# Starting both feature groups of a recurrence's input projection on x's first two chunks, and turning six of x's eight chunks with VectorE blocks

## The chip, the cores and the metric

The kernel runs on one core of one Trainium2 chip. The metric is the device time of one execution in microseconds (us); lower is better. A core has five engines that run their own instruction streams and wait for each other through semaphores: TensorE (PE, matrix multiply; its weight loads are listed as PEld), VectorE (DVE), ScalarE (ACT), GpSimd (POOL) and SyncE (SP, which here only issues transfers). Transfers run on 16 DMA engines, which all queues share.

## The reference, cut to what matters

One layer of a hybrid encoder: an RMS norm of x, one wide projection, attention on one part of it, a gated linear recurrence (LRU) on another, a gated mix, and an output projection. x is 512 tokens by 2048 features, all float32.

```python
h = rms_norm(x, norm_w)
proj = jnp.einsum('bsd,de->bse', h, w_in)
q, k, v, g_attn, xr, g_lru = jnp.split(proj, SPLITS, axis=-1)
attn_out = attention_group(q, k, v, q_norm_w, k_norm_w)
lru_out = lru_group(xr, conv_w, conv_b, lru_wa, lru_ba, lru_wx, lru_bx, lru_lambda)
mixed = jnp.concatenate([rms_norm(attn_out, attn_norm_w) * jax.nn.silu(g_attn),
                         rms_norm(lru_out, lru_norm_w) * jax.nn.silu(g_lru)], axis=-1)
return x + jnp.einsum('bse,ed->bsd', mixed, w_out)
```

The change touches only the start: the projection to `xr`, the recurrence's input (1024 features, split into two groups of 512).

## The kernel before, in words

**Products.** Every float32 factor is held as two parts, a rounded high part and a low rest, and a product is three matmuls (`mm3`, L152 to L155): high by high, high by low, low by high. `wsplit` (L216) makes the two parts of a piece of weights: ScalarE writes `wh` (L223), VectorE writes `wl` (L224). x's two parts are kept as tiles named `x` (tag `x2`), 16 high and 16 low ones, each 128 features by 512 tokens. The norm's row factor is not in them: it is the vector `rbc`, multiplied in when a group's sums leave the accumulators.

**Chunks.** x's 2048 features are worked through in eight chunks of 256 (two slices of 128, called k). A chunk of x is loaded by `xload` (L245) with tokens on the partitions, as a tile named `b`, and must be turned so that features lie on the partitions. There are two ways. For the first `TURNED` = 5 chunks `xturn` (L254) has TensorE transpose eight 128x128 blocks against the identity `ident` (L258); ScalarE takes the high part out of the accumulator (L263) and VectorE the low part (L266). For chunks 5, 6 and 7 VectorE transposes 32x32 blocks in four instructions (`blocks`, L286) into a tile `xu`; `put_aside` (L294) writes it to DRAM (`xd`) in one transfer, and `bring_back` (L301) reads it in four transfers into another `xu` so that the blocks lie in order; ScalarE scales it by `norm_w` (L343) and writes the high part, VectorE the low part (both L344). `xsquare` makes the sums of squares for the norm, on VectorE for the first five chunks (L277), on ScalarE for the others (L273).

**The first group.** `proj_feat` (L385) runs over the chunks; per chunk 24 matmuls of 128x512 go into the four accumulators of the group. For the first two chunks the matmuls stand in an order of their own (L394), so that each starts as soon as its part is there. It yields after every 6 matmuls, and at such a step `moves` (L1206) says which loads, turns and splits are written there. Group 1 (`a1`) is done over all eight chunks; then group 2 (`a2`) over all eight, woven with the recurrence of group 1 (`lru_half`), then the projection to keys and values, woven with the recurrence of group 2.

**What sets the order.** TensorE's program is in the order written, throughout. At the start the same holds for SP (the `with` of `s1`, L1171), and for ScalarE and VectorE up to step (1, 2) (`s2`, closed at L1236); elsewhere a planner orders an engine's instructions by priorities. Each engine, and SP as the queue of the transfers, runs its program in order: an instruction that waits holds up those behind it. A raw weight tile `wr` comes from a ring of three, the split parts `wh` and `wl` from four buffers each. There are two sets of four accumulator banks, `pj` and `mm`.

**Small things at the start.** GpSimd makes the identity `ident` (a memset and a select out of `make_identity`, listed under masks.py) and a few constants. `norm_w` comes in as 16 rows, `nw_st`, and is turned by one transpose (`columns`, L194). `vec_load` (L185) loads seven small vectors (104 rows of 128 numbers) into `vec_st`, which is turned in the same way.

Of the kernel before, what the change touches and what calls it, by code (L numbers as in the profile page):

```python
# [11 lines left out]
F32 = mybir.dt.float32  # L12
# [40 lines left out]
TURNED = 5  # L53
# [10 lines left out]
def hybrid_kernel(  # L64
# [172 lines left out]
    highs, x_parts, squared = {}, [], []  # L237
# [16 lines left out]
    def xturn(xc, kk, then=None):  # L254
        pt = mm()
        for t in range(NT):
            ks = slice(kk % 2 * P, (kk % 2 + 1) * P)
            nc.tensor.transpose(pt[:, t * P : (t + 1) * P], xc[:, t, ks], ident)  # L258
        if then:
            then()  # L260
        xh[kk], xl[kk] = x2(), x2()
        with behind(split_done[-1] if kk > 3 else ()):
            highs[kk // 2] = nc.scalar.activation(  # L263
                xh[kk], pt, AF.Identity, scale=nw[:, kk : kk + 1]
            ).ins
        nc.vector.scalar_tensor_tensor(  # L266
            xl[kk], pt, nw[:, kk : kk + 1], f(xh[kk]), op0=ALU.mult, op1=ALU.subtract
        )

    def xsquare(xc, c):  # L270
        for t in range(NT):
            if c >= TURNED:
                nc.scalar.activation(  # L273
                    xc[:, t, :], xc[:, t, :], AF.Square, accum_out=ssq[:, t, c : c + 1]
                )
                continue
            square = nc.vector.scalar_tensor_tensor(  # L277
                xc[:, t, :], xc[:, t, :], 1.0, xc[:, t, :], op0=ALU.mult, op1=ALU.mult,
                accum_out=ssq[:, t, c : c + 1],
            )  # L280
            if c == 1:
                squared.append(square.ins)
# [25 lines left out]
    def xchunk(c):  # L308
        with tc.high_priority(AHEAD):
            (xc,) = xload(c)  # L310
        yield
        if c < TURNED:
            with tc.high_priority(AHEAD):
                for k in range(2):
                    xturn(xc, 2 * c + k)
            if c == 2:
                yield
            with behind(split_done[2][1:] if c == 2 else ()):
                xsquare(xc, c)
            yield  # L320
            return
        u, back = (
            ring.tile([P, NQ, 2, NT, B], F32, name=nm("xu")) for ring in (aring, hring)
        )
        with tc.high_priority(AHEAD), tc.issue_after(squared[-1] if c == TURNED else split_done[3][1]):
            for t in range(NT):
                blocks(u, t, xc[:, t, :])
        yield
        with tc.high_priority(AHEAD):
            there = put_aside(u, "xd", KT // 2 - TURNED)  # L330
        with tc.issue_after(highs[TURNED - 1]):
            xsquare(xc, c)
        yield
        with tc.high_priority(AHEAD):
            bring_back(back, there)
        yield
        with tc.high_priority(AHEAD), behind(split_done[-1]):
            for k in range(2):
                kk = 2 * c + k
                xh[kk], xl[kk] = x2(), x2()  # L340
                hi, lo = (in_order(v) for v in (xh[kk], xl[kk]))
                v = back[:, :, k]
                nc.scalar.activation(v, v, AF.Identity, scale=nw[:, kk : kk + 1])  # L343
                x_parts[:] = nc.scalar.copy(hi, v).ins, nc.vector.tensor_sub(lo, v, f(hi)).ins  # L344
        yield
# [11 lines left out]
    def rows(dst, col, dg):  # L357
# [14 lines left out]
        pb = mm()  # L372
# [4 lines left out]
    def xstats():  # L377
        s = const([P, NT], "xsum")
        nc.vector.reduce_sum(s, ssq, axis=AX.X)
        rsqrt_mean(rstd, s, DM, NT)  # L380
        yield from rows(rbc, rstd, lambda: k2(F32R, (P, NT, P)))
# [3 lines left out]
    def proj_feat(c0, acc, first=None, given={}, take=None):  # L385

        acc += [pj() for _ in range(4)]
# [93 lines left out]
    def lru_half(half, acc):  # L481
# [11 lines left out]
        xrs = evac_bc(acc)  # L493
        for b in range(0, 4, 2):
            bs = slice(b, b + 2)
            steps = ((6, 4, 8, 4), (10, 5, 8, 5))[half][bs]
            yield from lru_pair(4 * half + b, xrs[bs], grs[bs], steps, 99 if half and b else 0)

    def lru_pair(n0, xrs, grs, steps, rest):
# [23 lines left out]
        for b, n in enumerate((n0, n0 + 1)):  # L523
# [4 lines left out]
            for dst, j0, bias in ((rs[b], 0, R_BA), (is_[b], 2, R_BX)):  # L528
                for d in range(2):
                    pg = mm()  # L530
# [641 lines left out]
    s1.enter_context(tc.manual_schedule(engines={mybir.EngineType.SP}))  # L1172
# [5 lines left out]
    with tc.high_priority():  # L1178
# [12 lines left out]
        xturn(xc, 0, split_first)  # L1191
        busy(WARM2)
    stats = xstats()
    chunks = [xchunk(c) for c in range(1, KT // 2)]

    raws = {}

    def fetch_x(c):
        with tc.high_priority(AHEAD):
            (raws[c],) = wraw(w_in, c * 2 * P, C_XR)  # L1200

    def split_x(c):
        with tc.high_priority(AHEAD), behind(x_parts):
            given[c] = [wsplit(raws[c], k) for k in range(2)]

    moves = {  # L1206
# [6 lines left out]
    }  # L1213

    def move(step):
        for name in moves.get(step, "").split():
            n = int(name[1])
            if name[0] == "x":
                next(chunks[n - 1])
            else:  # L1220
                (fetch_x if name[0] == "w" else split_x)(n)

    for step in proj_feat(C_XR, a1, first, given):
        if step is None:
            with tc.high_priority():
                first.append(wsplit(raw, 1, nc.vector.tensor_copy))
                xturn(xc, 1)
            xsquare(xc, 0)
            move(None)
            given[1] = wload(w_in, 2 * P, C_XR)  # L1230
            continue
        c, e = step
        move(step)
        if (c, e) == (1, 2):
            s2.close()
        if (c, e) == (4, 2):  # L1236
            with tc.high_priority(AHEAD):
                vec_load()
        if (c, e) == (7, 1):
            columns(vec, vec_st)  # L1240
        if (c, e) in ((4, 3), (KT // 2 - 1, 0)):
            with tc.high_priority(AHEAD), tc.issue_after(split_done[-1][1]):
                next(stats)

# [3 lines left out]
    fill = proj_feat(C_XR + SEQ, a2)  # L1248
# [9 lines left out]
    fill = with_sums(fill, 8, 16)  # L1258
    weave(fill, lru_half(0, a1))
# [200 lines left out]
```

## Time and profile before

| | us |
|---|---|
| median of 3 runs | 626.39 (626.31 to 626.44) |
| profiled execution | 626.48 |
| its span on the core | 624.7 |
| TensorE busy | 620.0 (99%), 2756 matmuls |
| VectorE, ScalarE, GpSimd busy | 495.3, 352.4, 101.8 |
| mean transfer rate over the span | 204 GB/s |

The profiled execution is 1.8 us longer than its span (what lies before and after) and within 0.1 us of the median. All times in views are counted from the span's start. A row of a timeline has the start, the duration, the engine, the line of the kernel, the operation, what it writes and reads, and how many instructions it merges.

### The profile page before, as it was taken

Reading aid. Unit: us, or ns where it says so; the run is one execution under the profiler, and the core shown is the slowest. Engines: PE = TensorE matmul, PEld = TensorE weight load, DVE = VectorE, ACT = ScalarE, POOL = GpSimd, SP = SyncE. Lnnn points to the kernel's source line nnn. Section 1 sums busy time; section 2 is a strip of 40 time slices with the busy share of each in tenths; the row PEclk is TensorE's granted clock in tenths of the full one; section 3 lists DMA queues with packets and bytes.
Section 4 is the critical chain, followed back from the end, with each engine's and each line's share of the span. In section 5 each row is a group of like instructions: output and inputs, shape, how many; then the busy total and the mean of one; then the engine's idle time right before and its main releaser. Section 6 shows DMA issues by size and latency. Waiting matters only on the chain.

```text
span 624.7 us, 8293 instructions
## 1 busy us (share of the span) xinstructions
PE 620.0 (99%) x2756; PEld 512.6 (82%) x2756; DVE 495.3 (79%) x800; ACT 352.4 (56%) x617; POOL 101.8 (16%) x135
## 2 busy tenths in 40 slices
PE   9999999999999999999999999999999999999997
PEld 7888888888888888888888888888888888888886
DVE  5958979986699876887887888549979866887776
ACT  3675799479946833545485548338345633443441
POOL 0000210112003622622123223100210101010010
PEclk9999999999999999999999999999999999999999
DMA  8878686759774599479659646932995777897252
GB/s 285 277 210 271 178 202 171 175 135 195 239 235 137 170 247 240 100 204 270 192 173 258 201 137 192 256 91 76 283 254 184 216 250 242 288 333 230 68 202 101
DMA packets 74026, 127.61 MB, mean 204 GB/s; under 512 B 6664, under 2 KB 29312, under 8 KB 73984
## 3 DMA queue, kind: packets, MB, share of 16 engines
q1 hardware_dynamic: 66096, 109.65, 56.7%
q0 software_dynamic: 7712, 17.31, 14.3%
q8 instruction: 21, 0.34, 0.2%
q14 instruction: 21, 0.17, 0.1%
q10 hardware_dynamic: 176, 0.14, 0.1%
HBM read 110.29 MB, written 37.75 MB: 237 GB/s over the span
## 4 chain that ended last, share of the span: by engine, by line
PE 99%; DVE 0%; issue 0%
PE pj L154 20%; PE pj L155 20%; PE pj L153 20%; PE mm L1040 14%; PE pj L1040 11%; PE mm L155 4%; PE mm L154 3%; PE mm L153 3%; PE pj L394 2%; PE mm L258 1%; PE mm L1167 1%; PE mm L836 0%; DVE cb L1069 0%; PE mm L194 0%; PE mm L373 0%; DVE ones L159 0%
## 5 line engine op out<-in xcount | busy, mean ns | idle before, releaser
L153 PE MATMUL pj<-x,wh 128*128 128x512 f32 x368 | 143.5, 390 | 0.0
L155 PE MATMUL pj<-x,wl 128*128 128x512 f32 x368 | 143.2, 389 | 0.0
L154 PE MATMUL pj<-x,wh 128*128 128x512 f32 x368 | 143.2, 389 | 0.0
L223 ACT CAST wh<-wr 128x512 fp32r<-128x512 f32 x142 | 84.5, 618 | 81.5 <-PE pj L154 29.8
L224 DVE TENSOR_TENSOR wl<-wr,wh 128x512 fp32r<-128x512 f32 x144 | 98.5, 712 | 20.5 <-ACT wh L223 19.2
L888 ACT CAST wh<-wr 128x1024 fp32r<-128x1024 f32 (+1 forms) x72 | 60.6, 860 | 75.3 <-PE mm L1040 36.0
L889 DVE TENSOR_TENSOR wl<-wr,wh 128x1024 fp32r<-128x1024 f32 (+1 forms) x72 | 68.6, 983 | 29.0 <-ACT wh L888 28.9
L153 PEld LDWEIGHTS pj<-x,wh 128*128 128x128 f32 x368 | 69.1, 188 | 14.4
L154 PEld LDWEIGHTS pj<-x,wh 128*128 128x128 f32 x368 | 69.1, 188 | 14.3
L155 PEld LDWEIGHTS pj<-x,wl 128*128 128x128 f32 x368 | 69.1, 188 | 14.3
L154 PE MATMUL pj<-wl,x 128*128 128x512 f32 x192 | 74.7, 389 | 0.0
L155 PE MATMUL pj<-wh,x 128*128 128x512 f32 x192 | 74.7, 389 | 0.0
L153 PE MATMUL pj<-wh,x 128*128 128x512 f32 x192 | 74.7, 389 | 0.0
L912 POOL DMA_DIRECT2D t<-in_w_out_dram x40 | 33.6, 907 | 156.0 <-DMA t<-in_w_out_dram 96.9
L1040 PE MATMUL mm<-wh,ml 128*128 128x512 f32 x126 | 49.0, 389 | 0.0
L1040 PE MATMUL mm<-wh,mh 128*128 128x512 f32 x126 | 49.0, 389 | 0.0
L1040 PE MATMUL mm<-wl,mh 128*128 128x512 f32 x126 | 49.0, 389 | 0.0
L153 PEld LDWEIGHTS pj<-wh,x 128*128 128x128 f32 x192 | 36.0, 188 | 7.6
L154 PEld LDWEIGHTS pj<-wl,x 128*128 128x128 f32 x192 | 36.0, 188 | 7.5
L155 PEld LDWEIGHTS pj<-wh,x 128*128 128x128 f32 x192 | 36.0, 188 | 7.4
L712 POOL TENSOR_SCALAR p<-p,sm 128x512 f32<-128x512 f32 x32 | 24.2, 761 | 89.4 <-DVE sm L711 89.4
L1040 PE MATMUL pj<-wl,mh 128*128 128x512 f32 (+1 forms) x100 | 38.5, 385 | 0.0
(205 smaller groups left out, 1052.9 us busy)
## 6 DMA issues: line engine op xcount, KB each, us to landing
wr<-in_w_in_dram SPq DMA_DIRECT2D x71, 512.0 KB, 5.0
wr<-in_w_out_dram SPq DMA_DIRECT2D x21, 512.0 KB, 5.1
t<-in_w_out_dram POOLq DMA_DIRECT2D x40, 256.0 KB, 7.1
wr<-t SPq DMA_DIRECT2D x40, 256.0 KB, 5.8
pd<-u SPq DMA_DIRECT2D x16, 512.0 KB, 3.0
pt<-pd SPq DMA_DIRECT2D x64, 128.0 KB, 4.1
t<-in_w_out_dram SPq DMA_DIRECT2D x24, 256.0 KB, 5.3
wr<-in_w_out_dram SPq DMA_DIRECT2D x22, 256.0 KB, 4.2
```

The costliest lines, as they stand in the source:

```text
L153: nc.tensor.matmul(acc, lh, rh, start=start, stop=False)
L154: nc.tensor.matmul(acc, lh, rl, start=False, stop=False)
L155: nc.tensor.matmul(acc, ll, rh, start=False, stop=stop)
L223: copy(hi, raw[:, k, :]).ins,
L224: nc.vector.tensor_sub(lo, raw[:, k, :], f(hi)).ins,
L258: nc.tensor.transpose(pt[:, t * P : (t + 1) * P], xc[:, t, ks], ident)
L394: nc.tensor.matmul(acc[e], w[:, e * P : (e + 1) * P], x_[2 * c + k], start=c == k == j == 0, stop=False,)
L712: last_pool[0] = nc.gpsimd.tensor_scalar(p, p, sm, 0.0, op0=ALU.mult, op1=ALU.add).ins
L888: nc.scalar.copy(hi[:, to], b)
L889: nc.vector.tensor_sub(lo[:, to], b, f(hi[:, to]))
L912: nc.gpsimd.dma_start(dst, src, accum_op=ALU.add)
L1040: nc.tensor.matmul(dst[s][:, es], lh[:, ts_], rh[:, es], start=i == ends_[0] and j == 0, stop=i == ends_[1] and j == 2,)
```

## The change

- Two chunks instead of five are transposed by TensorE (`TURNED` = 2); chunks 2 to 7 go through VectorE's blocks, DRAM and back. Their sums of squares are made on ScalarE.
- After group 1's matmuls on chunks 0 and 1, group 2's matmuls on chunks 0 and 1 stand in TensorE's program (eight steps of 6 matmuls, drawn from `fill` by `islice`), then group 1's chunks 2 to 7, then group 2's. For this group 2 has the accumulators `mm` and group 1's gates `pj`.
- `vec_load` issues its seven loads from GpSimd's queue, where `moves` has the letter G, instead of SP's at step (4, 2); GpSimd's program is in the order written as well (`s1`). The vectors are turned at step (1, 3), and the recurrence's constants follow early on VectorE.
- ScalarE's and VectorE's programs are in the order written up to step (6, 0). The table `moves` now has a letter for each act (loads of x L, of weights W and F, turning T and H, squares Q, splits S and P, blocks B, put aside D, bring back R, making the parts V, the norm Z).
- The norm's broadcast takes a bank of `pj`, freed by a copy of the first accumulator (`done`).

```diff
-TURNED = 5
+TURNED = 2
...
-            nc.sync.dma_start(vec_st[lo : lo + src.shape[0], :], src)
+            nc.gpsimd.dma_start(vec_st[lo : lo + src.shape[0], :], src)
...
+    def block_x(c):
+        units[c] = [ring.tile([P, NQ, 2, NT, B], F32, name=nm("xu")) for ring in (aring, hring)]
+        for t in range(NT):
+            blocks(units[c][0], t, chunk[c][:, t, :])
+    def aside_x(c):
+        units[c][0] = put_aside(units[c][0], "xd", KT // 2 - TURNED)
+    def back_x(c):
+        bring_back(units[c][1], units[c][0])
+    def whole_x(c):
+        for k in range(2):
+            v = units[c][1][:, :, k]
+            nc.scalar.activation(v, v, AF.Identity, scale=nw[:, 2 * c + k : 2 * c + k + 1])
+        for k in range(2):
...
+            nc.scalar.copy(hi, v)
+            nc.vector.tensor_sub(lo, v, f(hi))
...
-        pb = mm()
+        pb = pj()
...
-    s1.enter_context(tc.manual_schedule(engines={mybir.EngineType.SP}))
+    s1.enter_context(tc.manual_schedule(engines={mybir.EngineType.SP, mybir.EngineType.Pool}))
...
+    def vectors(_):
+        with tc.issue_after(split_done[-1][1]):
+            vec_load()
...
+        None: "Q0 L1 W1 S1 L2 F0 L3 F1 G0",
+        (0, 2): "T1 H1 H1 B2 D2 P0 L4 L5 R2",
...
+    fill = proj_feat(C_XR + SEQ, a2, given=next_given, bank=mm)
+    done = []
     for step in proj_feat(C_XR, a1, first, given):
...
+        if step == (1, 3):
+            columns(vec, vec_st)
+            for c, e in itertools.islice(fill, 8):
+                move((c, e, 1))
...
-    fill = with_sums(fill, 8, 16)
-    weave(fill, lru_half(0, a1))
+    fill = with_sums(fill, 8, 8)
+    weave(fill, lru_half(0, a1, done))
```

GpSimd's program, from its first instruction of the kernel proper. Before:

```order
masks.py:197 MEMSET ident 128x128
L163 MEMSET ones_r 128x128
masks.py:199 ISA
masks.py:199 AFFINE_SELECT ident<-ident 128x128
L165 MEMSET nhalf 128x48
```

And after:

```order
L185 DMA vec_st<-in_conv_w_dram 32x128
L185 DMA vec_st<-in_conv_b_dram 8x128
L185 DMA vec_st<-in_lru_ba_dram 16x128
L185 DMA vec_st<-in_lru_bx_dram 16x128
L185 DMA vec_st<-in_lru_lambda_dram 16x128
L185 DMA vec_st<-in_attn_norm_w_dram 8x128
L185 DMA vec_st<-in_lru_norm_w_dram 8x128
masks.py:197 MEMSET ident 128x128
L163 MEMSET ones_r 128x128
masks.py:199 ISA
masks.py:199 AFFINE_SELECT ident<-ident 128x128
```

The seven loads stand ahead of the two instructions that make the identity, and wait for nothing; the planner put them there, though the code writes them later.

SP's program where the first chunk is put aside and brought back. `xd` is the DRAM tile, `xu` the tile in blocks (the source of `xd`) and in order (its reader), `b` a chunk of x, `wr` raw weights. Before, with chunk 5's `xd` first, then those of 6 and 7:

```order
L294 DMA xd_405<-xu_337 128x1024
L211 DMA wr_411<-in_w_in_dram 128x2x512
L301 DMA xu_338<-xd_405 32x4x256 x4
L211 DMA wr_417<-in_w_in_dram 128x2x512
L294 DMA xd_437<-xu_425 128x1024
L294 DMA xd_443<-xu_431 128x1024
L301 DMA xu_426<-xd_437 32x4x256 x4
L211 DMA wr_489<-in_w_in_dram 128x2x512
L301 DMA xu_432<-xd_443 32x4x256 x4
```

And after, for chunks 2, 3, 4 and the put-aside of 5:

```order
L294 DMA xd_255<-xu_249 128x1024
L244 DMA b_42_265<-in_x_dram 128x4x256
L244 DMA b_43_267<-in_x_dram 128x4x256
L301 DMA xu_250<-xd_255 32x4x256 x4
L294 DMA xd_295<-xu_289 128x1024
L211 DMA wr_297<-in_w_in_dram 128x2x512
L301 DMA xu_290<-xd_295 32x4x256 x4
L244 DMA b_52_327<-in_x_dram 128x4x256
L294 DMA xd_354<-xu_348 128x1024
L211 DMA wr_382<-in_w_in_dram 128x2x512
L301 DMA xu_349<-xd_354 32x4x256 x4
L294 DMA xd_414<-xu_408 128x1024
```

Six chunks instead of three go this way, one behind the other: each chunk's four reads wait for its own write, and the next chunk's write and weights stand behind those reads.

TensorE's program at the seam between the two groups, after the change. `pj` are group 1's accumulators, `mm_54` group 2's first, `wh_23` chunk 1's weights for group 1 and `wh_38` chunk 0's for group 2:

```order
L398 MATMUL pj_12_167<-x2_34_244,wh_23_198 128x512
L398 MATMUL pj_13_168<-x2_34_244,wh_23_198 128x512
L194 MATMUL mm_53_335<-ident_84,vec_st_97 128x104
L153 MATMUL mm_54_338<-x2_8_156,wh_38_257 128x512
L154 MATMUL mm_54_338<-x2_9_157,wh_38_257 128x512
```

48 matmuls of group 2 stand here between group 1's chunks 1 and 2; before, group 1's chunk 2 followed.

More of the change, by code (lines that the diff above doesn't have):

```diff
@@ L261, in xturn @@
         xh[kk], xl[kk] = x2(), x2()
[L262 to L265, printed above, removed]
+        yield
+        nc.scalar.activation(xh[kk], pt, AF.Identity, scale=nw[:, kk : kk + 1])
+        yield
         nc.vector.scalar_tensor_tensor(
@@ L268, in xturn @@
         )
+        yield
     def xsquare(xc, c):
@@ L306, in in_order @@
         return v.rearrange("p (t i r) -> p i t r", t=NT, i=NQ)
[L308 to L345, printed above, removed]
@@ new lines, in hybrid_kernel, with load_x, turn_x, step_x @@
+    chunk, squares, halves, units = {}, {}, {}, {}
+    def load_x(c):
+        (chunk[c],) = xload(c)
+        squares[c] = xsquare(chunk[c], c)
+    def turn_x(c):
+        halves[c] = [xturn(chunk[c], 2 * c + k) for k in range(2)]
+        step_x(c)
+    def step_x(c):
+        for half in halves[c]:
+            next(half)
+    def square_x(c):
+        drain(squares[c])
+    def block_x(c):
+        units[c] = [ring.tile([P, NQ, 2, NT, B], F32, name=nm("xu")) for ring in (aring, hring)]
+        for t in range(NT):
+            blocks(units[c][0], t, chunk[c][:, t, :])
@@ L380, in xstats, with proj_feat @@
         rsqrt_mean(rstd, s, DM, NT)
+        yield
         yield from rows(rbc, rstd, lambda: k2(F32R, (P, NT, P)))
-    def proj_feat(c0, acc, first=None, given={}, take=None):
-        acc += [pj() for _ in range(4)]
+    def proj_feat(c0, acc, first=None, given={}, take=None, bank=pj):
+        acc += [bank() for _ in range(4)]
         for c in range(KT // 2):
@@ L479, in evac_bc, with lru_half @@
         return res
-    def lru_half(half, acc):
+    def lru_half(half, acc, done=()):
         grs = []
@@ L496, in lru_half, with lru_pair @@
             steps = ((6, 4, 8, 4), (10, 5, 8, 5))[half][bs]
-            yield from lru_pair(4 * half + b, xrs[bs], grs[bs], steps, 99 if half and b else 0)
-    def lru_pair(n0, xrs, grs, steps, rest):
+            yield from lru_pair(4 * half + b, xrs[bs], grs[bs], steps, 99 if half and b else 0, mm if half else pj)
+    def lru_pair(n0, xrs, grs, steps, rest, bank):
         xcs, cs, rs, is_, ths = [], [], [], [], []
```

90 lines of the change are left out of this document (54 added, 36 removed), and 6 rows, old and new, of the table moves.

## Prediction

> **What bounds the kernel now.** I read the page first (engines, chain), then the chain in order of time, then the timelines of GpSimd, SP, ScalarE and VectorE over the first 60 us.
>
> ```profile
> PE 620.0 (99%) x2756; PEld 512.6 (82%) x2756; DVE 495.3 (79%) x800; ACT 352.4 (56%) x617; POOL 101.8 (16%) x135
> PE 99%; DVE 0%; issue 0%
> ```
>
> TensorE carries 99% of the chain. In order of time (start, duration, what):
>
> ```profile
> 1.04 2.74 PE mm L1167 x12
> 4.00 1.04 PE mm L258 x4
> 5.04 1.07 PE mm L1167 x5
> 6.11 1.22 PE pj L394 x4
> 7.33 0.44 PE mm L258 x4
> ...
> 10.99 0.87 PE mm L258 x8
> 11.87 4.13 PE pj L394 x18
> 16.00 0.87 PE mm L258 x8
> 16.88 2.77 PE pj L394 x12
> ...
> 23.29 0.87 PE mm L258 x8
> ...
> 468.62 2.72 PE mm L1040 x12
> ...
> 621.09 0.42 DVE cb L1069
> ```
>
> A matmul of 512 columns takes 2.72/12 = 0.227 us, a transpose 0.87/8 = 0.109. From 6.11 on one piece starts where the last ended: TensorE waits nowhere, so every transpose saved shortens the kernel, and every wait put in lengthens it one for one. The profiled execution, 626.48, is 0.1 over the median; the sum is made against 626.5.
>
> **Part 1: transposes removed.** L258 has 40 transposes; 16 are left. 24 x 0.109 = 2.6 us less on TensorE. The matmuls are the same in number.
>
> **Part 2: the identity comes later.** GpSimd now issues seven small loads ahead of `ident`, and TensorE's first transpose of data needs it.
>
> ```profile
> 0.72 0.20 POOL masks.py:197 MEMSET ident<- 128x128 f32 x1 [0.29 <-POOLq L1445]
> 1.11 0.29 POOL masks.py:199 TENSOR_SCALAR_AFFINE_SELECT ident<-ident 128x128 f32<-128x128 f32 x1
> 3.71 0.28 PE L194 MATMUL mm<-ident,nw_st 16*128 16x16 f32 x1
> ```
>
> Before, `ident` was ready at 1.40, and its first reader started at 3.71, when `norm_w` was there. What GpSimd pays for issuing a transfer:
>
> ```profile
> L912 POOL DMA_DIRECT2D t<-in_w_out_dram x40 | 33.6, 907 | 156.0 <-DMA t<-in_w_out_dram 96.9 <-issue 38.6 <-DMA t<-t 19.3
> L1109 POOL DMA_DIRECT2D wr<-in_x_dram x8 | 5.9, 743 | 56.7 <-DVE ml L867 32.4 <-DMA wr<-in_w_out_dram 13.6 <-issue 5.9
> L1064 POOL DMA_DIRECT2D out_dram<-cb x4 | 2.2, 540 | 1.3 <-DVE cb L1069 1.1 <-issue 0.2
> 62.80 1.10 POOL L912 DMA_DIRECT2D t<-in_w_out_dram  x1 [24.83 <-DMA t<-in_w_out_dram]
> ```
>
> No row has one as small as these (4 to 16 KB; 104 pieces of 512 bytes in all). The L1064 ones have 128 pieces, the L1109 ones 256: a line through 540 and 743 ns gives 0.34 us + 1.6 ns a piece, so seven cost 2.5 us: the low end. Seven at 0.907, with 0.2 for a first one (62.80 took 1.10), cost 6.5: the high end. I take 3.4: halfway between the line and seven times the shortest row (3.8), with 0.2 to 0.3 for the first. `ident` is then ready at 1.40 + 3.4 = 4.8, and everything behind TensorE's first transposes moves by 4.8 - 3.7 = **1.1 us** (0.2 to 4.2 at the ends). The transfers of x and weights are on SP and do not move.
>
> [...]
>
> **Part 3: chunks 2 to 7 by way of DRAM.** This adds 3 writes of 512 KB and 12 reads of 128 KB, all on SP, in a single file with the loads. Before:
>
> ```profile
> 17.78 0.34 SPq L294 DMA_DIRECT2D xd<-xu  x1
> 20.27 0.37 SPq L211 DMA_DIRECT2D wr<-in_w_in_dram  x1
> 26.18 1.76 SPq L301 DMA_DIRECT2D xu<-xd  x4
> 28.04 0.39 SPq L211 DMA_DIRECT2D wr<-in_w_in_dram  x1
> 28.52 1.26 SPq L294 DMA_DIRECT2D xd<-xu  x2
> 34.15 1.74 SPq L301 DMA_DIRECT2D xu<-xd  x4
> ```
> ```profile
> 31.31 1.34 ACT L343 ACTIVATE xu<-xu,nw 128x512 f32<-128x512 f32 x2 [1.71 <-DMA xu<-xd]
> 39.31 1.34 ACT L343 ACTIVATE xu<-xu,nw 128x512 f32<-128x512 f32 x2 [2.98 <-DMA xu<-xd]
> 40.56 1.13 ACT L344 CAST x<-xu 128x512 fp32r<-128x512 f32 x2
> 41.59 1.14 ACT L223 CAST wh<-wr 128x512 fp32r<-128x512 f32 x2
> ```
>
> Four reads take 31.31 - 26.18 = 5.1 us from first issue to the scaling that waits for them, and again 39.31 - 34.15 = 5.2. From one set of reads to the next, with weights and two writes between, SP needed 34.15 - 26.18 = 8.0 us: the second set waits for the first of the two writes, which had to queue behind reads and weights. Where the write is first in the file, a load less is ahead of it. What one load takes in a full queue:
>
> ```profile
> 32.00:34.00 2.00, 2.00 (x10) 1.68 (x9) 1.33 (x5) 2.00 (x7) 0.00 (x0) 1.00 0.98 399
> pd<-u SPq DMA_DIRECT2D x16, 512.0 KB, 3.0
> ```
>
> At 399 GB/s 512 KB take 1.3 us; so the step is about 6.6 us with the write first (chunks 3, 5, 6, 7) and 8.0 with a load of x ahead of it (chunk 4). The other end is the second row: such a write lands after 3.0 us when little else runs; with 1.8 us to issue four reads that makes a step of 4.8.
>
> The first write waits for chunk 1's low parts and then chunk 2's blocks on VectorE:
>
> ```profile
> 12.33 1.40 DVE L266 SCALAR_TENSOR_TENSOR x<-mm,nw,x 128x512 fp32r<-128x512 f32 x2
> 16.32 1.43 DVE L286 STREAM_TRANSPOSE xu<-b 128x256 f32<-128x256 f32 x4 [1.22 <-DMA b<-in_x_dram]
> ```
>
> 12.33 + 1.40 + 1.1 + 1.43 = 16.3 for its issue; landed about 3.5 later (nearer 3.0, since the file is short there) at 19.8; two loads of x stand behind it and ahead of the reads, which costs the first step some 0.3. The reads of chunk 7 are issued at 19.8 + 0.3 + 4 x 6.6 + 8.0 = 54.5 and landed at 59.6. ScalarE scales (1.34), makes two high parts (1.13) and splits weights (0.6 for the first): matmuls from 62.6 on.
>
> When does TensorE want chunk 7? It starts at 6.11 + 1.1 = 7.2, needs 48 matmuls (10.9) and 12 transposes (1.3) for chunks 0 and 1 and 0.1 for the vectors: 19.5; 10.9 for group 2's two chunks: 30.4; 5 chunks of 24 x 0.227 = 5.44: 57.6. So chunk 7 is **5.0 us late** in all, about half of it already at chunk 4, whose weights stand behind a write and a load of x. With steps of 4.8 nothing is late; with 8.0 throughout, 10 us. I take 5.0, since the 8.0 is measured in this stage with these very transfers, and 3.0 us in another with little in the queue.
>
> **What costs nothing.** Chunks 2 to 4's squares move from VectorE to ScalarE, which sat idle 1.71 and 2.98 us before the two scalings above; that slack hides them, and if it is gone they delay the next chunk's parts by what exceeds it. The recurrence's constants are now ahead of chunk 2's low parts on VectorE:
>
> ```profile
> 64.24 0.17 DVE L455 TENSOR_SCALAR lc<-lc 128x16 f32<-128x16 f32 x1
> 64.44 0.18 DVE L457 TENSOR_TENSOR lc<-lc,lc 128x16 f32<-128x16 f32 x1
> ```
>
> 26 of them at 0.20 are 5.2 us, from about 24 to 29.4 (the start is an estimate: the vectors are turned at 19.5, and chunk 4's blocks and some 3 us of other work stand ahead); chunk 2 is wanted at 30.4, with its two low parts and two of weights (0.7 each, by the 1.40 for two above) behind them. The cover is group 2's 10.9 us; if it is short, up to 0.8. Later the recurrence of group 2 begins 48 matmuls sooner after that of group 1, while VectorE is full:
>
> ```profile
> 110.00:120.00 10.00, 10.00 (x46) 8.29 (x45) 10.00 (x14) 3.60 (x7) 1.66 (x2) 1.00 0.79 192
> ```
>
> The cover is the ten steps of 6 matmuls (13.6 us) between group 2's sums and its first gates; I take 0, and up to 2 for the range.
>
> **Sum.** 626.5 - 2.6 + 1.1 + 5.0 = **630.0**.
>
> **Rivals.**
> - *The file keeps up.* If a write behind reads lands about as fast as in the attention (3.0), steps are 4.8 to 5.4, no longer than a chunk's 5.44, and only the head is paid: 626.5 - 2.6 + 0.2 to 1.1 = 624.1 to 625.0. For it speaks that group 2's two chunks give 10.9 us of lead; against it the 8.0 us step. It decides from a mean step below 5.8: then chunk 7 is under 1.5 late and the 2.6 outweigh all.
> - *Partly late*, steps near 6: 1 to 2.5 us late, 626 to 627.5.
> - *TensorE's slow start happens longer.* Its first four transposes took 1.04 us against 0.44 for the next four; full pace came some 5 us after its first matmul (1.04 to 6.1). If the pause of 1.1 us that the late identity puts there starts this count again at 4.8, matmuls from 7.2 to 9.9 run at half pace: 1.4 more, 631.4. The profile's granted clock reads 1.00 throughout and cannot tell. [...]
> - *Both dear*: the identity 4 us late, or steps of 7.5: 633 to 636.
>
> **How the numbers follow.** The forecast (628 to 632 as its own range) 0.45; file keeps up 0.20; partly late 0.17; slow start 0.10; both dear 0.08. The measurement tells 0.2% (1.25 us) from no change. Faster by more: the second case, 0.20. Within: half of the third, 0.10. Slower: 0.70. For 8 in 10 the range leaves out the lower half of the second case and most of the last: 624.7 to 633.5.
>
> **What would show it.** Right: TensorE's chain has waits for `xu` or `wh` at chunks 4, 6 and 7 between 40 and 65 us, 5 in all; the first L394 matmul at about 7.2; seven GpSimd issues ahead of the memset, 0.35 to 0.6 each; 16 transposes at L258. Wrong, if SP's sets of reads follow each other by less than 5.8 us, if the seven issues end before 3 us or after 6, or if TensorE waits in the recurrence at 100 to 160 us.

## The result, and the profile after

The changed kernel takes 637.25 us (median of 4 runs, 635.83 to 638.38), the kernel before 626.41 beside it (626.31 to 626.44): ratio 1.0172, 95% interval 1.0151 to 1.0194. It is 10.8 us slower; the forecast was 3.5 slower, and the range ended at 633.5. The profiled execution of the changed kernel, the fastest of the four, took 635.83, its span 633.9. The page first, engine line and chain:

```profile
PE 621.3 (98%) x2732; PEld 510.7 (81%) x2732; DVE 496.0 (78%) x788; ACT 361.2 (57%) x648; POOL 105.6 (17%) x142
PE 82%; DMA 6%; DVE 6%; ACT 3%; issue 1%; POOL 1%; SPq 1%; ACTq 0%; POOLq 0%
```

The matmuls are 24 fewer, as they should be. TensorE has 82% of the chain instead of 99%, though it is still busy for 98% of the span: at its few waits the chain leaves it and runs back through the transfers and the other engines that made it wait. The head on GpSimd (first and last of the seven issues, and the select that makes the identity) and on TensorE:

```profile
1.27 0.67 POOL L185 DMA_DIRECT2D vec_st<-in_conv_w_dram  x1 [0.84 <-POOLq L1472]
...
4.45 0.51 POOL L185 DMA_DIRECT2D vec_st<-in_lru_norm_w_dram  x1
...
5.33 0.30 POOL masks.py:199 TENSOR_SCALAR_AFFINE_SELECT ident<-ident 128x128 f32<-128x128 f32 x1
```
```profile
5.69 0.23 PE L194 MATMUL mm<-ident,nw_st 16*128 16x16 f32 x1 [1.91 <-POOL ident masks.py:199]
5.86 0.66 PE L258 MATMUL mm<-ident,b 128*128 128x128 f32 x4
...
7.29 1.19 PE L398 MATMUL pj<-x,wh 128*128 128x512 f32 x4 [0.23 <-ACT x L263]
...
9.69 2.00 PE L398 MATMUL pj<-x,wh 128*128 128x512 f32 x8
```

Seven issues from 1.27 to 4.96; the first matmul with weights starts at 7.29. In the kernel before it is 6.11 in the chain, which counts from the end of the piece ahead, and 5.82 in the timeline; the first row of eight matmuls starts at 9.69 instead of 8.53, so from there on the shift is 1.16. SP's file (start, duration, line, what): each `xd` is a chunk put aside, each `xu<-xd ... x4` a chunk brought back.

```profile
16.11 0.34 SPq L294 DMA_DIRECT2D xd<-xu  x1
...
20.98 2.23 SPq L301 DMA_DIRECT2D xu<-xd  x4
...
27.76 1.74 SPq L301 DMA_DIRECT2D xu<-xd  x4
29.54 0.43 SPq L244 DMA_DIRECT2D b<-in_x_dram  x1
30.07 0.45 SPq L294 DMA_DIRECT2D xd<-xu  x1
30.57 0.43 SPq L211 DMA_DIRECT2D wr<-in_w_in_dram  x1
36.63 1.74 SPq L301 DMA_DIRECT2D xu<-xd  x4
...
42.37 1.75 SPq L301 DMA_DIRECT2D xu<-xd  x4
...
49.80 1.74 SPq L301 DMA_DIRECT2D xu<-xd  x4
51.64 0.38 SPq L294 DMA_DIRECT2D xd<-xu  x1
52.11 2.33 SPq L211 DMA_DIRECT2D wr<-in_w_in_dram  x2
55.19 2.99 SPq L301 DMA_DIRECT2D xu<-xd  x4
```

From set to set: 6.8, 8.9, 5.7, 7.4, 5.4; mean 6.84. Between 30.57 and 36.63 SP issues nothing: it stands at the reads until the write of 30.07 has landed. What TensorE makes of it, and what ScalarE waits for at chunk 7:

```profile
38.94 0.79 PE L153 MATMUL pj<-x,wh 128*128 128x512 f32 x1 [2.54 <-ACT wh L223]
39.53 0.63 PE L154 MATMUL pj<-x,wh 128*128 128x512 f32 x1
...
47.69 0.50 PE L153 MATMUL pj<-x,wh 128*128 128x512 f32 x1 [1.60 <-ACT wh L223]
...
66.79 0.50 PE L153 MATMUL pj<-x,wh 128*128 128x512 f32 x1 [0.59 <-ACT wh L223]
...
163.88 0.50 PE L153 MATMUL mm<-k,k 128*128 128x512 f32 x1 [0.81 <-ACT b L536]
```
```profile
63.85 1.34 ACT L341 ACTIVATE xu<-xu,nw 128x512 f32<-128x512 f32 x2 [4.98 <-DMA xu<-xd]
```
```profile
30.00:35.00 5.00, 5.00 (x24) 4.09 (x23) 3.05 (x8) 3.88 (x13) 0.00 (x0) 1.00 0.93 280
35.00:40.00 5.00, 2.46 (x10) 1.65 (x9) 2.22 (x4) 2.07 (x6) 0.00 (x0) 0.86 0.64 202
40.00:45.00 5.00, 5.00 (x19) 4.05 (x18) 2.84 (x7) 3.39 (x10) 0.00 (x0) 0.80 1.02 339
45.00:50.00 5.00, 3.40 (x12) 2.12 (x11) 2.33 (x6) 2.98 (x11) 0.00 (x0) 0.88 0.95 279
50.00:55.00 5.00, 5.00 (x19) 4.00 (x18) 2.98 (x6) 5.00 (x15) 0.01 (x1) 0.78 0.75 234
```

Three waits at chunks 3, 4 and 7 (2.54, 1.60 and 0.75 with the 0.16 that follows) and one in the recurrence (0.81). Column 2 of the windows is TensorE, and the last three numbers are the granted clock, the busy share of the transfer engines and GB/s. At 40 to 45 TensorE is "busy" all 5 us and yet has only 19 matmuls, where the window of full pace at 30 to 35 has 24 (with those that reach in from either side); the granted clock says why, 0.80. After 2.54 and after 1.60 us of waiting some 3 us of matmuls follow each other by 0.43 instead of 0.227. Summed from start to start, less 0.227 each, the slow matmuls of chunks 3 and 4 cost 3.5 us (3.9 in the expectation of e1, which counts the intervals at the waits with them). It looks like a cause; e1 shows that here it is none.

### The profile page after: what moved, and what is told of

Its sections match the earlier page's. It is cut to its first block, busy times and chain, and to the rows that moved or that the text cites. A ratio compares the mean times of both kernels' runs of the same rounds, so it can differ in the third digit from the quotient of the medians.

```text
span 633.9 us, 8298 instructions
## 1 busy us (share of the span) xinstructions
PE 621.3 (98%) x2732; PEld 510.7 (81%) x2732; DVE 496.0 (78%) x788; ACT 361.2 (57%) x648; POOL 105.6 (17%) x142
## 4 chain that ended last, share of the span: by engine, by line
PE 82%; DMA 6%; DVE 6%; ACT 3%; issue 1%; POOL 1%; SPq 1%; ACTq 0%; POOLq 0%
PE pj L155 15%; PE pj L153 15%; PE pj L154 15%; PE mm L1044 14%; PE pj L1044 11%; PE mm L153 4%; PE mm L155 4%; PE mm L154 4%; DMA xd<-xu 2%; DMA xu<-xd 2%; DMA b<-in_x_dram 1%; DVE wl L224 1%; DVE k L519 1%; PE pj L398 1%; DMA t<-in_w_out_dram 1%
## 5 line engine op out<-in xcount | busy, mean ns | idle before, releaser
L153 PE MATMUL pj<-x,wh 128*128 128x512 f32 x304 | 120.0, 395 | 4.7 <-ACT wh L223 4.7
L155 PE MATMUL pj<-x,wl 128*128 128x512 f32 x304 | 119.6, 393 | 0.2 <-DVE wl L224 0.2
L154 PE MATMUL pj<-x,wh 128*128 128x512 f32 x304 | 119.5, 393 | 0.0
L153 PEld LDWEIGHTS pj<-x,wh 128*128 128x128 f32 x304 | 57.8, 190 | 17.8 <-ACT wh L223 6.0
L155 PEld LDWEIGHTS pj<-x,wl 128*128 128x128 f32 x304 | 57.7, 190 | 13.4 <-DVE wl L224 1.2
L154 PEld LDWEIGHTS pj<-x,wh 128*128 128x128 f32 x304 | 57.9, 190 | 12.1
```

Of the source, the lines that this page charges most:

```text
L153: nc.tensor.matmul(acc, lh, rh, start=start, stop=False)
L154: nc.tensor.matmul(acc, lh, rl, start=False, stop=False)
L155: nc.tensor.matmul(acc, ll, rh, start=False, stop=stop)
```

## The experiments

Each kernel ran beside the kernel before (626.2 to 626.5 in each set).

| kernel | us, median (range) | ratio to before, 95% |
|---|---|---|
| the change | 637.25 (635.83 to 638.38) | 1.0151 to 1.0194 |
| e1 waits filled | 638.17 (636.64 to 638.82) | 1.0166 to 1.0197 |
| e2 reads by GpSimd | 639.38 (635.13 to 640.52) | 1.0192 to 1.0229 |
| e3 reads wait for no write | 632.08 (630.00 to 632.93) | 1.0063 to 1.0103 |
| e4 identity first | 635.03 (634.07 to 636.01) | 1.0119 to 1.0152 |
| e5 e4, group 2's third load behind | 631.95 (630.96 to 634.73) | 1.0072 to 1.0120 |
| e6 e4, groups one after the other | 643.35 (642.49 to 644.58) | 1.0257 to 1.0287 |
| e7 e4, 3 chunks by TensorE | 630.84 (629.53 to 632.51) | 1.0047 to 1.0081 |
| e8 e4, 4 chunks by TensorE | 628.53 (627.55 to 630.16) | 1.0025 to 1.0053 |
| e9 e5, weights ahead of writes | 639.45 (637.64 to 640.92) | 1.0192 to 1.0231 |
| e10 e9, more steps | 641.33 (640.87 to 641.71) | 1.0225 to 1.0253 |
| e11 e5, writes first | 631.75 (630.67 to 634.33) | 1.0079 to 1.0117 |
| e12 e11, 3 chunks by TensorE | 625.97 (625.84 to 628.83) | 0.9993 to 1.0010 |
| e13 e12, one step moved | 626.15 (625.95 to 626.70) | 0.9990 to 1.0008 |
| e14 before, identity late | 630.51 (629.69 to 631.52) | 1.0049 to 1.0076 |
| e15 pause at the head filled | 637.06 (634.99 to 639.24) | 1.0154 to 1.0196 |
| e16 e12, first half sooner | 627.57 (626.30 to 628.16) | 1.0006 to 1.0024 |
| e17 e16, second half later | 631.35 (629.87 to 631.81) | 1.0065 to 1.0090 |

**e1: is it the clock?**

```diff
+FILL = {(2, 3): 24, (3, 3): 32, (6, 3): 24}
...
+        for _ in range(FILL.get(step, 0)):
+            nc.tensor.matmul(
+                a1[0][:, : 2 * P], wv[:, :P], zero.bitcast(mybir.dt.bfloat16),
+                start=False, stop=False,
+            )
```

> The changed kernel with small TensorE products of zeros (256 columns, added to a sum: they change nothing) in the three places where TensorE waits: 24 ahead of chunk 3, 32 ahead of chunk 4, 24 ahead of chunk 7, at about 0.11 us each. The trace of the changed kernel has waits of 2.54, 1.60 and 0.75 us there, and after the first two some 3.4 us of matmuls at 0.43 instead of 0.227 us, which adds 3.9. Theory 'late file': chunk 7's start, 66.9 us, is set by SyncE's single file and the landing of its reads, and the slow matmuls only use up time that TensorE would have waited; so the granted clock returns to 1.00 and the time stays at 636 to 638. Rival 'slow clock': the 3.9 us of slow matmuls come on top of the waits; with TensorE kept busy they go, and the time falls to about 633.4.

Measured 638.17. In its windows the clock is back and the time is not:

```profile
40.00:45.00 5.00, 5.00 (x29) 3.92 (x27) 2.64 (x7) 4.64 (x14) 0.00 (x0) 1.00 0.99 312
45.00:50.00 5.00, 5.00 (x39) 4.18 (x38) 1.49 (x3) 1.34 (x3) 0.00 (x0) 1.00 1.08 298
```

From SP's first write to the scaling of chunk 7 it is 65.74 - 18.38 = 47.4 us, in the changed kernel 63.85 - 16.11 = 47.7. The time itself says little here: in this run TensorE was slow at the head (four matmuls in 2.08 us from 7.80) and the file began 2.3 us later, and the fill ahead of chunk 7 was too long, so that the first matmul came 69.89 - 65.74 = 4.2 us after the scaling instead of 2.9. The file's length does say something: it is the same with and without the slow matmuls. At full pace TensorE arrives sooner and has longer to wait (here filled); chunk 7's data set the end, and the slow matmuls in the middle are absorbed.

**e2 and e3: SP's standing still, or the traffic?** e2 gives the reads to GpSimd's queue; e3 leaves them on SP and reads from x, so that they wait for no write (what it computes is then not the layer).

```diff
-        bring_back(units[c][1], units[c][0])
+        bring_back(units[c][1], units[c][0], nc.gpsimd)      # e2
+        bring_x(units[c][1])                                 # e3: same pieces, from x
```

> The changed kernel with the 24 reads that bring chunks 2 to 7 back issued by GpSimd, which is idle there, instead of SyncE. Theory 'late file': SyncE stands still at each set of reads until the write before it has landed (3.6 to 6.6 us each), and loads stand behind; with the reads elsewhere no wait is left between 30 and 70 us: 626.5 - 2.6 (transposes) + 1.2 (head) + 1.1 (recurrence) = 626.2, say 625.5 to 627.5. Rival 'traffic': the write and the reads in 1 KB pieces fill the transfer engines (busy share 0.9 to 1.1 at 40 to 65 us), so the chunks are late whoever issues them: 633 to 637.

> The changed kernel with the reads of chunks 2 to 7 taken from x itself, in the same pieces, so that they wait for no write; the writes stay, the traffic is the same, and the numbers computed are not the reference's. Theory 'late file': no wait is left between 30 and 70 us, 625.5 to 627.5. Rival 'traffic': 633 to 637, with waits at chunks 3, 4 and 7 as before.

e2 was no faster, 639.38, over both ranges (its profile is of the fastest run, 635.13). SP no longer stood at the reads, but a write issued at 25.01 between two loads let GpSimd's reads start only at 35.03, and SP's next write, which needs VectorE's blocks of a later chunk, then came at 37.32:

```profile
25.01 0.34 SPq L294 DMA_DIRECT2D xd<-xu  x1
25.45 0.39 SPq L211 DMA_DIRECT2D wr<-in_w_in_dram  x1
37.32 0.34 SPq L294 DMA_DIRECT2D xd<-xu  x1
```
```profile
35.03 2.21 POOL L301 DMA_DIRECT2D xu<-xd  x4 [4.96 <-DMA xd<-xu]
```

That is 10 us from a write's issue to its landing, with the transfer engines at a busy share of 1.07 between 25 and 35 us. e3 came to 632.08: neither theory's number. About half of the loss went with the waiting for writes (5.2 us), about half stayed. In its profile, with the same bytes moving, TensorE still waits 0.70, 0.94, 0.39 and 0.19 us for weights; part of the rest is a head about 1.1 us slower than in the changed kernel's profile (its first row of eight matmuls starts at 10.77). So neither theory does alone, and both together fit: a file that stands at every write, in front of queues that are nearly full (busy shares of 1.08 to 1.10 between 30 and 45 us in e3).

**e4: identity first.**

```diff
-    make_identity(nc, ident)
+    with tc.high_priority(2 * AHEAD):
+        make_identity(nc, ident)
```

> The changed kernel with the identity made ahead of GpSimd's seven loads. TensorE's first matmul of weights returns from 7.29 to about 6.1 us. Theory 'late file': the file begins with VectorE's work behind the first transposes, so it moves with the head and the time falls by 1.0 to 1.2 (636.1). Rival 'x sets the file': the file starts when x's third chunk has landed, not with the head; then the waits at chunks 3 to 7 grow by what the head gains and the time stays at 637.0 to 637.5.

635.03, 2.2 less, with intervals of 1.0 to 1.3 us on each side, so the 1.2 of the shift is within it. In its trace the first matmul with weights starts at 5.82, SP's first write at 15.02 (16.11 before), chunk 7's scaling at 61.91 (63.85): the file moves with the head.

**e5: what stands ahead of the last reads.** In the changed kernel two loads are issued at 52.11: chunk 6's weights, and group 2's third load, which the planner put there.

```diff
-        (4, 2): "V6 W7 Z0",
+        (4, 2): "V6 W7 F2 Z0",
-        (6, 0): "S7",
+        (6, 0): "S7 P2",
```

> e4 (identity first, 635.0) with the third chunk of group 2's weights (512 KB), which SyncE loads ahead of the last set of reads, put behind chunk 7's weights. Theory 'file and traffic': chunk 7 waits both for SyncE's standing still and for what is ahead in full transfer queues; 512 KB less ahead at 260 to 300 GB/s bring chunk 7's reads 1.7 to 2.0 us sooner, and since chunk 7's start sets the end, 633.0 to 633.5. Rival 'file alone': that load runs while SyncE waits for chunk 7's write anyway; 634.5 to 635.5.

631.95: 3.1 less, more than expected. Chunk 7 no longer waits:

```profile
52.73 2.41 SPq L302 DMA_DIRECT2D xu<-xd  x4
```
```profile
58.97 1.34 ACT L342 ACTIVATE xu<-xu,nw 128x512 f32<-128x512 f32 x2 [2.58 <-DMA xu<-xd]
```

6.2 us from the reads' issue to the scaling, where it had been 8.7. What is left are the waits for weights at chunks 3 and 4 (1.62 and 2.79).

**e6: the change without the interleave.** Group 2 after group 1, its two early loads out of the file, the rest as e4.

```diff
-        None: "Q0 L1 W1 S1 L2 F0 L3 F1 G0",
+        None: "Q0 L1 W1 S1 L2 L3 G0",
...
-            for c, e in itertools.islice(fill, 8):
+            for c, e in itertools.product(range(2), range(4)):
```

> e4 with the other part of the change undone: group 2 begins after group 1, and two chunks only are turned by TensorE. Theory 'file and traffic': chunk 7 comes at the earliest 5 us sooner (three loads of group 2's weights, 1.5 MB, are out of the queue) and 48 matmuls (10.9 us) are left for later instead of filling the wait: 640 to 645. Rival 'interleave crowds': the 1.5 MB of group 2 in the queue are what makes the chunks late; without them 625 to 630.

643.35, as expected. TensorE waits 9.13 us at chunk 2, which the 48 matmuls of group 2 had covered. So the parts are: two chunks by TensorE instead of five, +17.1 us; the interleave, -8.3; the late identity, +2.2.

**e7 and e8: fewer trips.**

```diff
-TURNED = 2
+TURNED = 3      # e7; 4 in e8, with its own table
...
-        (0, 2): "T1 H1 H1 B2 D2 P0 L4 L5 R2",
-        (1, 0): "Q2 B3 D3 W2 Q1",
+        (0, 2): "T1 H1 H1 P0 L4 L5",
+        (1, 0): "T2 H2 H2 B3 D3 W2 Q1",
...
```

> e4 with chunk 2 turned by TensorE too: 8 transposes more (0.9 us), one trip less, so one step of SyncE's file (6.8 us on the mean) and 1 MB of traffic less. Theory 'file and traffic': chunk 7, which is some 8 us late in e4, is at most 1 us late: 626.5 - 1.7 + 1.1 (recurrence) + 0 to 1 = 626 to 627. Rival 'weights': chunk 3's and 4's weights are late by themselves, because they stand behind writes; 630 or more.

> e4 with chunks 2 and 3 turned by TensorE: 32 transposes, four trips, weights of chunk 2 early. Theory 'file and traffic': nothing is late, 626.5 - 0.9 + 1.1 (the wait of the recurrence at 163 us stays) = 626.2 to 627.2. Rival 'weights': 629 or more.

630.84 and 628.53, both slower than the theory's range: e7 is in the rival's, e8 just under it. Each chunk less by way of DRAM gives 2 to 4 us. e7 still waits 2.50 us for weights at 44 us and 1.40 for chunk 7, with group 2's third load ahead of the reads as in e4.

**e9, e10 and e11: the order in the file.** e9 puts each chunk's weights ahead of the next write; e11 the other way round puts the loads of x behind the writes.

```diff
-        (1, 2): "P1 R3 L6",
+        (1, 2): "P1 R3 W3 L6",     # e9
+        (1, 2): "P1 R3",           # e11
...
-        (0, 2, 1): "V2 W3 R4",
+        (0, 2, 1): "V2 R4",        # e9
+        (0, 2, 1): "V2 W3 L6 R4",  # e11
...
```

> e5 (632.0) with the weights of chunks 3 to 6 each put one place ahead in SyncE's file, before the load of x and the write that stood ahead of them. In e5 TensorE waits 1.62 us at chunk 3 and 2.79 at chunk 4, both for weights whose parts come last, with some 2.4 us of slow matmuls behind, while the chunks' own data were scaled 4 to 6 us earlier. Theory 'order in the file': the weights come 1.3 to 5 us sooner, the reads 1.3 us later, no wait over 0.5 us is left before 100 us: 626.5 - 2.6 + 1.1 (recurrence) = 625.0, say 624.5 to 627. Rival 'the queues are full': whatever is put first makes the other late, waits of the same sum stand at the chunks' own data: 630.5 to 633.

e9 was the worst miss: 639.45, 7.5 us slower than e5. Its sets of reads, and the stretch before the last:

```profile
19.98 1.86 SPq L302 DMA_DIRECT2D xu<-xd  x4
...
36.43 1.75 SPq L302 DMA_DIRECT2D xu<-xd  x4
...
62.02 1.74 SPq L302 DMA_DIRECT2D xu<-xd  x4
```
```profile
60.00:65.00 5.00, 2.29 (x5) 1.38 (x6) 3.76 (x9) 2.13 (x5) 0.00 (x0) 0.64 0.34 101
```

Five steps take 42.0 us, 8.4 each, against 6.7 in e5; at 60 to 65 the transfer engines are busy for a third of the time. A write with a load just ahead of it lands later: in e9 the reads that wait for such a write start 6.9, 6.0, 5.8 and 6.8 us after its issue; in e5 it is 4.7, 4.1, 5.2 and 3.7 us where the write stands right behind the reads before, and 6.2 where a load stands between. Standing at the reads, SP issues nothing (39.66 to 44.77 in e9).

> e9 with 8 instead of 5 steps of other matmuls between the first and the second block of gates in the recurrence's second half, where TensorE waits 0.8 us for ScalarE to empty a bank. If that wait comes from group 2's recurrence beginning 48 matmuls sooner, it and the 0.3 us of slow start behind it go: 1.1 us under e9, 623.9 where e9 gives 625.0. Rival: ScalarE is full there (9.9 of 10 us at 150 to 170 us), so the wait moves to a later block and the time is e9's within 0.3.

e10 (steps 10, 8 in place of 10, 5) was 641.33, 1.9 slower than e9, and so in neither range: the block's wait fell to 0.36 (at 172 us), and a new one of 0.67 came at 221 us, again for ScalarE. These two are 1.03 against 0.87 in e9, so they do not explain the 1.9.

> e5 (632.0) with nothing left ahead of a write: the loads of x's chunks 6 and 7 go behind the writes and the weights of chunks 3 and 4. It is e9 the other way round: there one load more ahead of each write made the mean step between two sets of reads 8.4 us instead of 6.6 in e5, and the time 639.4. Theory 'what stands ahead of the write is paid in the step, what stands behind it runs in SyncE's wait': steps of 6.0 to 6.3, the waits at chunk 3 (1.62) and chunk 4 (2.79) fall below 1 in all and the slow matmuls behind them go: 626.5 - 2.6 + 1.1 (recurrence) = 625.0, with what is left 625 to 628. Rival 'traffic': the same bytes pass in the same time, steps stay at 6.6 and the time within 1 of 632.

e11: 631.75, e5 again; steps 6.6. Loads behind the write do not shorten the step; that the reads and the next write then stand behind them in the transfer queues would explain it, but was not shown. The rival's number.

**e12: e11 with one trip less.**

> e11's order with chunk 2 turned by TensorE as well (three chunks by TensorE, five by way of DRAM; e7 was that in the old order, 630.8): one step and 1 MB less for 8 transposes (0.9 us). Theory 'what stands ahead of the write': chunk 7 has a step of spare time and nothing is late: 626.5 - 1.7 + 1.1 = 625.9, say 625.5 to 627. Rival 'traffic': like e7 with the third load behind, 629 to 630.

625.97, as expected, 0.3 under the kernel before in the median and not to be told from it (0.9993 to 1.0010). All of TensorE's waits over the span:

```profile
PE mm L1173 <- DVE ones L159: 1.0, 1, 1.0
PE mm L153 <- ACT b L538: 0.8, 1, 0.8
```

The first is the start. Between 2 and 150 us nothing waits, with the transfers at a busy share of 0.93 over 25 to 60 us. Its steps are 7.1 us, longer than a chunk's 5.44; what it has is one step less and the lead of the 48 matmuls. e7 has both too and is 4.9 us slower; it has a load of x ahead of one of its writes, and group 2's third load ahead of the last reads. Which of these counts, or how much, was not separated.

**e13, e16 and e17: the recurrence's wait.**

```diff
-            steps = ((6, 4, 8, 4), (10, 5, 8, 5))[half][bs]
+            steps = ((6, 4, 8, 4), (10, 6, 7, 5))[half][bs]    # e13
+            steps = ((6, 4, 6, 4), (10, 5, 8, 5))[half][bs]    # e16
+            steps = ((6, 4, 6, 4), (11, 6, 6, 5))[half][bs]    # e17
```

> e12 (626.0, nothing late before 150 us) with one step of six matmuls (1.36 us) moved from behind the second block of gates in the recurrence's second half to ahead of it; the sum of the steps stays (e10 had added three). Theory: the block waits 0.85 us for ScalarE to empty the first bank and 0.28 go with the start; 1.36 us later the bank is empty: 1.1 us less, 624.8 to 625.2. Rival: ScalarE is full there and the next block waits instead, 625.7 to 626.3.

> e12 (626.0) with the second pair of gates of the recurrence's first half two steps of six matmuls (2.7 us) sooner. Theory 'ScalarE's first-half work comes too late': its tanh, exp and square roots end up to 2.7 us sooner, the wait of 0.85 us at 154 us and the 0.28 behind it go: 624.8 to 625.2. Rival 'ScalarE is full': it is busy without a gap from 136 us on, the gates' inputs come no sooner, the wait stays: 625.8 to 626.3.

> e16 with the first blocks of the second half one step, and the second blocks two steps, later (the sum of the steps stays 28). Theory as for e16, with 2.7 us more of distance: no wait at all, 624.6 to 625.2. Rival 'ScalarE is full': the wait goes on to the next block, 625.8 to 626.5.

None gained: 626.15, 627.57, 631.35; e16 and e17 are slower than either of their ranges. In e16 the wait at 154 us is gone and stands in the first half instead, again for ScalarE to empty a gate's bank:

```profile
99.34 0.50 PE L153 MATMUL pj<-k,k 128*128 128x512 f32 x1 [0.24 <-ACT b L538]
101.48 0.50 PE L153 MATMUL pj<-k,k 128*128 128x512 f32 x1 [1.17 <-ACT b L538]
```

In e17 these two stay and a wait of 2.07 us for the same line comes back at 158 us. So ScalarE's work for the recurrence takes what it takes; with 48 matmuls less of other work beside it some block waits. e6, which has these 48 in their old place, has no wait there. A version that beats both kernels was not found.

**e14 and e15: the head.** e14 is the kernel before with `vec_load` on GpSimd's queue and nothing else; e15 the changed kernel with WARM 22 instead of 12.

> The kernel before with only the seven small loads issued by GpSimd, which puts them ahead of its identity; TensorE's order is the same. Theory 'shift': everything behind the first transposes moves by 1.1 to 1.2 us: 627.4 to 627.6, spread as before (0.4). Rival 'shift and slow clock': the pause of 1.9 us brings half pace back in some runs: 628 to 630, spread of 1 us or more.

> The changed kernel with 22 instead of 12 products ahead of the first transposes, so that TensorE's pause of 1.9 us at 3.8 us is about filled while the identity stays late. Theory 'the head's pause costs clock': no slow matmuls at 5 to 13 us in any run, so VectorE's and SyncE's work behind the first chunks starts at the same time in all: 635.5 to 636.3, and the spread falls below 1.5. Rival 'shift only': 636.8 to 637.7 with the spread unchanged.

e14 takes 630.51, 4.3 us more than the kernel before and over both ranges, for one word in the code. TensorE's rows there, and behind them those of the kernel before for the four transposes and the first eight matmuls in a row:

```profile
5.70 0.28 PE L194 MATMUL mm<-ident,nw_st 16*128 16x16 f32 x1 [1.91 <-POOL ident masks.py:199]
...
7.80 2.08 PE L394 MATMUL pj<-x,wh 128*128 128x512 f32 x4
...
10.38 1.93 PE L394 MATMUL pj<-x,wl 128*128 128x512 f32 x4
12.15 1.99 PE L394 MATMUL pj<-x,wh 128*128 128x512 f32 x8
```
```profile
3.93 1.11 PE L258 MATMUL mm<-ident,b 128*128 128x128 f32 x4
...
8.53 2.00 PE L394 MATMUL pj<-x,wh 128*128 128x512 f32 x8
```

After the pause of 1.91 us four matmuls take 1.9 to 2.1 us, until about 12; then eight take as long. That eight starts at 12.15 instead of 8.53, 3.6 us late, of which the shift alone is 2.0; no chunk is late there to hide it. More came later (TensorE waits 0.38 us for ScalarE at 97 us). In e15 the pause is 0.62 and there are no slow matmuls at the head, yet it takes 637.06, the rival's number, with a spread of 4 us; nor has the changed kernel's profiled execution slow matmuls there, after the same 1.91 us. So a slow head is not needed for a long time. In e15's profiled execution (638.69) chunk 7 starts at 67.60, after a wait of 1.59 us, and half pace follows, nine matmuls from 68.83 to 72.47 (3.64 us, 2.04 at 0.227 each): with no later chunk to wait for, the 1.6 us that it costs count in full. That the spread comes from the file, as late landings and as half pace behind the last of them, is argued: it is about 1 us in 10 of e12's 11 runs and in all of e13's, where nothing waits for the file.

## Why the prediction was wrong

Right in direction; the loss was 10.8 us instead of 3.5. By its own steps, against the profiled 635.83:

- *Transposes, -2.6.* Right: 16 are left, and the matmul count fell by 24.
- *Identity, +1.1.* The number was right, by luck. The issues took 0.48 to 0.67 us (0.35 to 0.6 forecast) and the identity was there at 5.6, not 4.8, so TensorE's first transposes began 2.0 us late. But in this execution it ran at full pace behind the pause (four transposes in 0.66 us, 1.11 before) and won 0.8 back: the first matmul with weights came at 7.29 (7.2). The step can have a second price, put down as a rival of 0.10 with 1.4 us: the half pace of the start goes on longer. The profiled execution did not pay it; e14 did, 3.6 us at the head and 4.3 in all, and so did e1's.
- *SP's steps, 6.6 and once 8.0.* Right in the mean, 6.84 against 6.88, and the last reads were issued at 55.19 (54.5). The single steps were 5.4 to 8.9, so errors either way cancel.
- *Landing of the last reads, 5.1. **This is the step that failed.*** ScalarE could scale only 8.7 us after their issue. From there the working held: 63.85 + 3.07 = 66.9 for the first matmuls, and TensorE's row says 66.79. The 5.1 was read off the kernel before, where one load stood ahead of such reads; here two did, and group 2's third load had no price in the sum. e5 takes that one away: 6.2 instead of 8.7, and 3.1 us of the time. The other traces agree: with two loads between the last write and the last reads ScalarE scaled 8.8 (e4), 8.6 (e7) and 7.9 us (e6) after the reads' issue, with one 6.2 (e11) and 4.5 (e12), with none 4.4 (e9). Chunk 7 came 66.8 - 57.6 = 9.2 us late, not 5.0.
- *Where the lateness shows.* Half right. The chunk's place was given as 4, for weights behind a write and a load of x; the first wait is at chunk 3, whose weights stand behind just such a pair (29.54 to 30.57), then 4, then 7. The waits add up to 4.9 and the forecast said 5.0: a coincidence. Counted from start to start, less 0.227, the gaps are 5.2 and the half pace 3.5, and chunk 2 started 0.35 behind the forecast: together 9.1 of the 9.2. By e1, where the file is as long without half pace, the waits would be longer by as much.
- *The cover on ScalarE and VectorE.* Held: the constants ended at 29.1 (29.4 forecast), and chunk 2 did not wait.
- *The recurrence, taken at 0, up to 2.* 1.1: 0.81 of wait, at 163.88, and 0.3 of a slower start. Group 2's gates come sooner, and ScalarE has not emptied the first bank. e6 has no such wait.

The sum with the measured terms: 626.5 - 2.6 + 1.2 + 9.2 + 0.6 (the second wait and the slow first matmuls at chunk 7) + 1.1 = 636.0; the profiled execution took 635.8. The median lies 1.4 above it, and for that no run shows the cause.

The rival "the file keeps up" fell with its own condition: the mean step was 6.84, and it needed under 5.8. "Both dear" (633 to 636) was the nearest, though the median lies above it too, and for another reason than it gave: the mean step was not 7.5, and the identity held up its first reader by 2 us, not 4.

## What to carry to other kernels

When a step is put into a queue's single file, price every transfer between the write and its reader, also those that a planner adds, and look for the last landing rather than the mean step: that is where the end was set here (8.7 us from the last reads' issue to the scaling with two loads ahead, 6.2 with one). A wait of TensorE that shows half pace behind it need not cost that half pace (SP's file took 47.7 us with it and 47.4 without); ask whether something later would be waited for anyway (fill the wait, with no more than the wait holds, and see). Behind the last wait it did cost (1.6 us in e15). And a small transfer moved to an idle engine is not free if that engine makes what the first matmul needs (4.3 us in e14).

## What the runs showed of the hardware

TensorE fell to half pace after waits of 2.54 and 1.60 us in the changed kernel; after 1.99 (e4), 1.62 (e5) and 2.50 us (e7) it did not. The length of the wait alone does not decide: half pace also followed waits of 2.62 (e4), 2.79 (e5), 3.04 and 9.13 (e6), and 2.31 and 1.59 us (e15), and did not follow 1.57 (e6), 1.58 (e11) and 2.03 us (e15). What else decides was not shown. In the changed kernel's record the granted clock is 0.50 in two stretches of 3.41 us, whose starts are 10.24 us apart:

```profile
38.57:41.98 3.41, 3.04 (x7) 2.42 (x8) 2.63 (x6) 3.30 (x12) 0.00 (x0) 0.50 0.94 293
48.81:52.22 3.41, 3.41 (x10) 2.64 (x9) 2.17 (x7) 3.41 (x11) 0.00 (x0) 0.50 0.52 177
```

In e15's timeline matmuls follow each other by 0.43 us from 48.53 to 51.52 and from 69.15 to 72.14, in e6's from 28.44 to 33.13 and from 47.13 to 50.13.

The profile's clock does not show the pace of the head. In e14 it reads 1.00 over 5 to 10 and over 10 to 15 us, and yet the first eight matmuls with weights take 2.08 and 1.93 us in fours, half the pace of the eight in 1.99 us behind them. Ahead of the pause twelve products of 256 columns take 2.74 us in the kernel before, the changed kernel and e14 alike; behind it the next five take 1.27 us in e14 and 0.71 in the changed kernel, and 1.27 in the kernel before, which has no pause there. So the pause at e14's head did not end a full pace: the products ahead of it took 0.23 us each, those at full pace behind the changed kernel's pause 0.14. Full pace came at about 12 us in e14, at about 7 in the kernel before and by 5.86 in the changed kernel, behind the same pause of 1.91 us; why it came so differently was not shown.

With chunks written out and 1 KB pieces read in, the transfer engines were busy to a share of 1.08 to 1.10 (e3, 30 to 45 us) at 295 to 324 GB/s; the kernel before moved 360 GB/s at a share of 1.04 between 10 and 25 us, with loads and one write. Which of the two, the writes or the reads, costs the difference was not separated.
